# Six of eleven gate passes of an MLP up-projection written as seven block products, and the normed x split before them

## The chip, the cores and the metric

The kernel runs on one core of a Trainium2 chip. The metric is the device time of one execution in microseconds (us), the median of several runs; less is better. Engines are named as in the profile: PE is TensorE (matmuls), PEld its weight loads, DVE is VectorE, ACT is ScalarE, POOL is GpSimd, SP is SyncE, which issues the big loads. Each engine executes its own instructions in order and waits on semaphores for the others.

## The reference

Two layers of a decoder trunk on 512 tokens of width 1024, all in float32. Layer 0 mixes tokens by windowed attention and a short convolution, layer 1 by gated linear attention (GLA). Each layer goes on with an MLP and a small gated embedding. The change is in the MLP:

```python
DFF = 2816
def _conv_ffn(h, w_up, conv_w, conv_b, w_down):      # h = rms_norm(x) : 512 x 1024
    u = _causal_depthwise_conv(h @ w_up, conv_w) + conv_b   # w_up: 1024 x 5632, width-3 taps over the tokens
    gate, up = jnp.split(u, 2, axis=-1)                     # 2816 gates, 2816 values
    return (jax.nn.gelu(gate, approximate=False) * up) @ w_down
def _rms_norm(x, gain):
    return x * rsqrt(mean(x * x) + 1e-6) * gain
```

## The kernel before

Activations lie transposed in SBUF: features on the 128 partitions, the 512 tokens along the free side. `self.xT[0..7]` is the residual, 8 tiles of 128 features. A float32 product is made of three matmuls on rounded parts: each operand is split into a high part (a cast by ACT) and a low part (the difference, by DVE), and `mm3` (L157 to L159) adds high·high, high·low and low·high in one bank of PSUM. Weights are split where they are loaded: `weights` issues the load on SP into a tile `raw` (two buffers), and `cut` makes `wh` (ACT, L137) and `wl` (DVE, L138) from it, 1024 elements per partition at a time (three buffers each). A product whose weights are not cut yet waits; so does a cut whose buffer still holds weights that PE reads.

The MLP (`ffn`, one call for each layer `i`) runs 11 passes `d`. A pass loads 256 gate columns and 256 value columns of `w_up` (1 MB each) and makes four column blocks of 128 features (two gates, two values), each with 8 x 3 matmuls of 128 weights columns by 512 tokens, into one bank from `ps()` (four banks; `pa()` gives four others). The rms factor is left out of the matmuls' input: `xg` holds split tiles of x·gain, and the token factor R (from `spread`, a tile of 128 x 512) is multiplied in when a bank is read. `taps` does that (L785), starts the convolution on ACT (L786) and adds two shifted multiples on DVE (L788). Then come Gelu (L810), the product of gate and value (L813) and its split into high and low part (L101, L102), which feeds the down projection:

```python
for w, ps, fo in ((wg, pss[0], f), (wv, pss[1], NF + f)):
    y = taps(ps, fo)
    if w is wg:
        nc.scalar.activation(y, y, AF.Gelu)
    got.append(y)
g, y = got
nc.vector.tensor_tensor(y, g, y, ALU.mult)
self.split(acts[f], y)
```

The factor R exists only some time after the first column: the squares of x are summed over partitions by PE (L323), and `spread` uses DVE, ACT and PE (L335 to L346).

The order of instructions on each engine is chosen at build time by a scheduler from priorities and its own estimates of durations; inside `manual_schedule(engines=...)` it is the written order for the engines named. Buffers are handed out at build time too, with waits for the last reader. After the MLP of layer 1 comes `ple1`, which already computes a product by seven blocks (L945 to L947), some of its matmuls 256 columns wide.

Of the kernel before, what the change touches and what calls it, by code (L numbers as in the profile page):

```python
# [9 lines left out]
F32 = mybir.dt.float32  # L10
F32R = mybir.dt.float32r
I32 = mybir.dt.int32
U8 = mybir.dt.uint8
AF = mybir.ActivationFunctionType
ALU = mybir.AluOpType
# [3 lines left out]
P = 128  # L19
S = 512  # L20
D = 1024
NT = S // P
ND = D // P
DFF = 2816
NF = DFF // P
# [3 lines left out]
ET = mybir.EngineType  # L29
LEVELS = (64, 32, 16, 8, 4, 2, 1)  # L30
CW = 512
TWO_PI = 2.0 * np.pi
PI_SAFE = 3.1415925

# [22 lines left out]
class Kernel:  # L57
# [140 lines left out]
    def columns(self, name, views, q=None):  # L198

        nc = self.nc  # L200
        n = sum(v.shape[0] for v in views)
        rows = self.sp.tile([P, P], F32, tag="vrow", name=self.nm("vrow"))
        if q is None and self.gate is not None:
            self.late(rows[:, :1])
        at = 0
        for v in views:
            (q or nc.gpsimd).dma_start(rows[at : at + v.shape[0], :], v)
            at += v.shape[0]
        if q:

            nc.scalar.copy(self.few(4, "rs", 4), self.mhalf[:, :4])
        col = self.cp.tile([P, -(-n // 64) * 64], F32, name=name)[:, :n]

        def finish():
            ps = self.pa()
            nc.tensor.transpose(ps[:, :n], rows[:n, :], self.ident[:n, :n])
            (nc.vector.tensor_copy if q else nc.scalar.copy)(col, ps[:, :n])
            return col

        return finish if q else finish()  # L220
# [109 lines left out]
    def spread(self):  # L330
# [7 lines left out]
        for i, x in enumerate((rh.bitcast(F32), rl)):  # L338
# [5 lines left out]
            nc.tensor.matmul(pr, self.ones_r, dg.rearrange("p a b -> p (a b)"), start=i == 0, stop=i == 1)  # L344
        R = self.sp.tile([P, S], F32, tag="R", name=self.nm("R"))
        nc.scalar.copy(R, pr)  # L346
        return R

# [31 lines left out]
    def rope_tables(self, pool):  # L380
# [16 lines left out]
        c2 = 4058 * 2.0**-21  # L397
        c3 = TWO_PI - c1 - c2
        magic = 1.5 * 2.0**23
        sc = []  # L400
        for name, quarter in (("sin", 0.0), ("cos", 0.25)):
            kk = pool.tile([P, NT * h], F32, tag="kk", name=f"kk{name}")
            o = pool.tile([P, NT, h], F32, name=f"tab{name}")
            r = o.rearrange("p a b -> p (a b)")
            nc.vector.tensor_scalar(kk, af, 1.0 / TWO_PI, quarter, op0=ALU.mult, op1=ALU.add)
            nc.vector.tensor_scalar_add(kk, kk, magic)
# [4 lines left out]
            if quarter:  # L411
                nc.vector.tensor_scalar_add(r, r, TWO_PI * quarter)
            nc.vector.tensor_scalar(r, r, PI_SAFE, -PI_SAFE, op0=ALU.min, op1=ALU.max)
# [21 lines left out]
    def mixer0(self):  # L435
        nc, a, tc = self.nc, self.a, self.tc
        with tc.tile_pool(name="m0", bufs=1) as mp:
# [236 lines left out]
            def conv_w(nme, j2):  # L674
                c0 = starts[nme] + 256 * j2
                return self.weights(w_in[:, :, c0 : c0 + 256], ND, 256)
# [26 lines left out]
            def conv_out(j2):  # L703
                for c in range(2):
                    xs, y = pre[c]
                    nc.vector.tensor_tensor(xs, pss["b", c], R, ALU.mult)
                    nc.vector.tensor_tensor(y, y, xs, ALU.mult)
# [5 lines left out]
            w = conv_w("x", 0)  # L713
            R = self.spread()
            qn0 = query(0)
# [5 lines left out]
            self.gate = None  # L721
            R2 = self.sp.tile([P, S], F32, tag="R", name="R2")
            nc.gpsimd.tensor_tensor(R2, R, R, ALU.mult)
# [43 lines left out]
            self.end_norm()  # L767


    def ffn(self, i, next_gain):  # L770
        nc, a, tc = self.nc, self.a, self.tc
        xg, R = self.xg, None
        wu = a["ffn_w_up"][i].rearrange("(k p) n -> p k n", p=P)
        w0, w1, w2, bb = self.fcv
        with tc.tile_pool(name=f"ffn{i}", bufs=1) as fp:
            acts = [self.pair(self.fp, "b0", "b1") for f in range(8)]
            for f in range(8, NF, 2):
                four = self.four(fp)
                acts += [(four[:, 0], four[:, 1]), (four[:, 2], four[:, 3])]

            def taps(ps, f):
                y = fp.tile([P, S], F32, tag="zt", name=self.nm("zt"), bufs=4)
                z = fp.tile([P, S + 2], F32, tag="z", name=self.nm("z"), bufs=3)
                nc.gpsimd.memset(z[:, :2], 0.0)
                nc.vector.tensor_tensor(z[:, 2:], ps, R, ALU.mult)  # L785
                nc.scalar.activation(y, z[:, 2:], AF.Identity, scale=w2[:, f : f + 1], bias=bb[:, f : f + 1])  # L786
                for tap, w in ((1, w1), (0, w0)):
                    nc.vector.scalar_tensor_tensor(  # L788
                        out=y, in0=z[:, tap : tap + S], scalar=w[:, f : f + 1], in1=y, op0=ALU.mult, op1=ALU.add
                    )  # L790
                return y

            for d in range(NF // 2):
                wg = self.weights(wu[:, :, 256 * d : 256 * d + 256], ND, 256)
                wv = self.weights(wu[:, :, DFF + 256 * d : DFF + 256 * d + 256], ND, 256)
                for c in range(2):
                    f = 2 * d + c
                    got = []
                    pss = []
                    for w in (wg, wv):  # L800
                        ps = self.ps()
                        for k in range(ND):
                            self.mm3(ps, w(k, c * P, (c + 1) * P), xg[k], start=k == 0, stop=k == ND - 1)
                        pss.append(ps)
                    if R is None:
                        R = self.spread()
                    for w, ps, fo in ((wg, pss[0], f), (wv, pss[1], NF + f)):
                        y = taps(ps, fo)
                        if w is wg:
                            nc.scalar.activation(y, y, AF.Gelu)  # L810
                        got.append(y)
                    g, y = got
                    nc.vector.tensor_tensor(y, g, y, ALU.mult)  # L813
                    self.split(acts[f], y)
            self.begin_norm(("a0", "a1"))
            done = self.residual(next_gain)
            if i == 1:
                self.forms = []
                scratch = lambda: fp.tile([P, S], F32, tag="zt", name=self.nm("gx"), bufs=4)

                def done(m, ps):
                    nc.vector.tensor_tensor(self.xT[m], self.xT[m], ps, ALU.add)
                    self.blocks(m, next_gain, scratch)

            self.project(self.rows(a["ffn_w_down"][i]), acts, ND, done)
            if i == 0:
                self.end_norm()
            else:
                self.ple1(fp)
# [69 lines left out]
    def ple1(self, fp):  # L899
# [3 lines left out]
        nc, a, tc = self.nc, self.a, self.tc  # L903
        forms = self.forms
        wg = a["ple_w_gate"][1].rearrange("(j u p) n -> u p j n", p=P, u=2)
        wp = a["ple_w_proj"][1].rearrange("(k p) n -> p k n", p=P)
        sl = lambda hl, t: (hl[0][:, t * P : (t + 1) * P], hl[1][:, t * P : (t + 1) * P])
        H, J = D // 2, ND // 2
# [40 lines left out]
        def back(hf, t):  # L949

            pb = self.pa()
            for q in range(4):
                nc.tensor.transpose(
                    pb[:, q * P : (q + 1) * P], self.xT[4 * hf + q][:, t * P : (t + 1) * P], self.ident
                )
            x = fp.tile([P, 512], F32, tag="zt", name=self.nm("xt"), bufs=4)
            nc.scalar.copy(x, pb)
            return x

# [10 lines left out]
        def result():  # L970
            return fp.tile([P, S + 2], F32, tag="z", name=self.nm("so"), bufs=3)[:, :S]
# [14 lines left out]
        def finish(hf, t, g, x, pj, s=None, c0=0, c1=H):  # L986
            if s is None:
                s = result()[:, c0:c1]
            nc.scalar.activation(s, g, AF.Sigmoid, scale=self.r[:, t : t + 1])
            nc.vector.tensor_tensor(s, s, pj[:, c0:c1], ALU.mult)  # L990
            nc.vector.tensor_tensor(s, s, x[:, c0:c1], ALU.add)
            nc.sync.dma_start(self.out[0, t * P : (t + 1) * P, hf * H + c0 : hf * H + c1], s)

        b11 = block(0, 0, True)
        w11 = chunks(b11)
        b12 = block(0, 1, True)
        pin = self.p_halves(1)
        b22 = block(1, 1, False)
        wj_raw = self.four(fp, F32)
        proj_load(1)  # L1000
        b21 = block(1, 0, False)
# [3 lines left out]
        X, Q = [[self.ps() for _ in range(2)] for _ in range(2)]  # L1005
        both = (0, H)
        with tc.manual_schedule(engines={ET.PE, ET.DVE, ET.Activation}):
# [3 lines left out]
            steps = [(j, i, both, Q[i]) for j in range(J) for i in range(2)]  # L1011
# [13 lines left out]
            steps = [(j, i, both, X[i]) for j in range(J) for i in range(2)]  # L1025
# [15 lines left out]
            steps = [(j, i, both, Q[i]) for j in range(J) for i in range(2)]  # L1041
# [8 lines left out]
            halves = ((0, H // 2), (H // 2, H))  # L1050
            Y = [Q[0]] + [y[:, : H // 2] for y in (Q[1], X[0])]
# [4 lines left out]
            steps = [(j, i, both, X[i]) for j in range(J) for i in range(2)]  # L1056
# [476 lines left out]
```

## Time and profile before

| | |
|---|---|
| median of 3 runs | 1247.56 us (1247.32 to 1248.36) |
| profiled execution, its own time | 1248.2 us |
| its span in the trace | 1246.4 us |
| PE busy | 1236.1 us, 5984 matmuls |
| DVE busy | 804.6 us, 1251 instructions |
| ACT busy | 561.5 us, 873 instructions |
| granted TensorE clock | 1.0 |
| `ps<-a,wh` etc., L157 to L159, 128x512 | 3 x 864 matmuls, the up-projection among them |
| `z<-ps,R` (L785), 128x512, DVE | 88, mean 687 ns |
| `zt<-z,vfb` (L786), 128x512, ACT | 88, mean 808 ns |
| `zt<-z,vfa,zt` (L788), 128x512, DVE | 176, mean 749 ns |
| `wh<-raw` (L137), 128x1024, ACT | 176, mean 1061 ns |
| `wl<-raw,wh` (L138), 128x1024, DVE | 176, mean 1224 ns |
| load of 1 MB of `w_up` | 44, median 5.1 us from issue to landing |

The span is the time from the first to the last instruction of one profiled execution; its own time also has what lies around the span. A duration in the trace is that of one instruction alone. Instructions of one engine overlap a little at their ends, so the time from start to start is shorter than the duration when they follow each other without a wait. In the timeline a row begins with the start (us from the span's start) and the duration, then engine, line, operation, output and inputs, shape and count, and in brackets the idle time before it and what ended it. In a row of windows there are the stretch, its length, busy time and count for PE, PEld, DVE, ACT and POOL, then the granted clock, the share of the DMA engines and GB/s.

### The profile page before, as it was taken

What the parts mean: (1) busy time and instruction counts of PE and PEld (TensorE: products, weight loads), DVE (VectorE), ACT (ScalarE), POOL (GpSimd) and SP (SyncE); (2) the same over time, 40 slices, a digit from 0 to 9 for tenths busy, and PEclk for the clock granted to TensorE, in tenths of its full rate; (3) what the DMA queues carried; (4) which work ended last, traced back from release to release, by engine and by line L of the source; (5) the groups of instructions that cost most, each with busy time, mean ns of one, the idle gap of its engine ahead of it and who ended that gap; (6) DMA issues with size and microseconds to landing.
All of it is one profiled execution on the core that took longest, in us unless ns stands there. A gap on an engine that the chain in (4) does not pass through costs nothing.

```text
span 1246.4 us, 15216 instructions
## 1 busy us (share of the span) xinstructions
PE 1236.1 (99%) x5984; PEld 1023.9 (82%) x5984; DVE 804.6 (65%) x1251; ACT 561.5 (45%) x873; POOL 52.1 (4%) x152
## 2 busy tenths in 40 slices
PE   9999999999999999999999999999999999999998
PEld 8877788888888888888987878888888888888887
DVE  6886556777777633346679875557777777444495
ACT  7466344444444322234563554335444444333374
POOL 2500000000000000000100000000000000000000
PEclk9999999999999999999999999999999999999999
DMA  6222232233333232223322222332223333322411
GB/s 214 92 80 56 83 102 83 88 100 102 101 102 101 83 103 93 93 74 103 111 91 68 69 68 68 101 110 95 83 94 102 101 101 102 101 93 94 149 46 68
DMA packets 111004, 117.45 MB, mean 94 GB/s; under 512 B 2728, under 2 KB 106210, under 8 KB 110932
## 3 DMA queue, kind: packets, MB, share of 16 engines
q1 hardware_dynamic: 109568, 115.35, 28.4%
q8 instruction: 47, 0.77, 0.2%
q0 software_dynamic: 560, 0.42, 0.2%
q10 hardware_dynamic: 804, 0.70, 0.2%
q14 instruction: 25, 0.20, 0.0%
HBM read 114.37 MB, written 2.10 MB: 93 GB/s over the span
## 4 chain that ended last, share of the span: by engine, by line
PE 88%; DVE 7%; ACT 2%; issue 1%; POOL 1%; DVEq 0%; ACTq 0%; POOLq 0%
PE ps L157 26%; PE ps L158 26%; PE ps L159 26%; DVE wl L138 1%; PE ps L947 1%; PE ps L946 1%; PE ps L945 1%; PE pa L1367 1%; PE pa L1344 0%; PE pa L595 0%; PE pa L158 0%; PE pa L192 0%; PE pa L159 0%; DVE F L1228 0%; PE pa L157 0%
## 5 line engine op out<-in xcount | busy, mean ns | idle before, releaser
L137 ACT ACTIVATE wh<-raw 128x1024 fp32r<-128x1024 f32 (+4 forms) x212 | 214.2, 1012 | 333.3 <-PE ps L158 298.7
L138 DVE TENSOR_TENSOR wl<-raw,wh 128x1024 fp32r<-128x1024 f32 (+4 forms) x212 | 246.5, 1164 | 153.2 <-ACT wh L137 152.1
L157 PE MATMUL ps<-a,wh 128*128 128x512 f32 x864 | 336.9, 390 | 0.0
L158 PE MATMUL ps<-a,wh 128*128 128x512 f32 x864 | 336.6, 390 | 0.0
L159 PE MATMUL ps<-a,wl 128*128 128x512 f32 x864 | 336.3, 389 | 0.0
L158 PEld LDWEIGHTS ps<-a,wh 128*128 128x128 f32 x864 | 162.3, 188 | 34.0 <-issue 0.3
L159 PEld LDWEIGHTS ps<-a,wl 128*128 128x128 f32 x864 | 162.2, 188 | 33.9
L157 PEld LDWEIGHTS ps<-a,wh 128*128 128x128 f32 x864 | 162.2, 188 | 33.7 <-issue 0.7
L788 DVE SCALAR_TENSOR_TENSOR zt<-z,vfa,zt 128x512 f32<-128x512 f32 x176 | 131.3, 749 | 3.6 <-ACT zt L786 0.6
L157 PE MATMUL ps<-b,wh 128*128 128x512 f32 x320 | 126.0, 395 | 0.5 <-ACT b L101 0.5
L159 PE MATMUL ps<-b,wl 128*128 128x512 f32 x320 | 125.7, 393 | 0.0
L158 PE MATMUL ps<-b,wh 128*128 128x512 f32 x320 | 125.0, 391 | 0.0
L785 DVE TENSOR_TENSOR z<-ps,R 128x512 f32<-128x512 f32 x88 | 60.3, 687 | 74.7 <-PE ps L159 74.7
L157 PE MATMUL ps<-four,wh 128*128 128x512 f32 x224 | 87.1, 389 | 0.0
L158 PE MATMUL ps<-four,wh 128*128 128x512 f32 x224 | 87.1, 389 | 0.0
L159 PE MATMUL ps<-four,wl 128*128 128x512 f32 x224 | 87.1, 389 | 0.0
L786 ACT ACTIVATE zt<-z,vfb 128x512 f32<-128x512 f32 x88 | 70.9, 808 | 5.0 <-DVE z L785 3.3
L157 PEld LDWEIGHTS ps<-b,wh 128*128 128x128 f32 x320 | 60.0, 188 | 14.0 <-ACT b L101 1.3
L159 PEld LDWEIGHTS ps<-b,wl 128*128 128x128 f32 x320 | 60.1, 188 | 12.5
L158 PEld LDWEIGHTS ps<-b,wh 128*128 128x128 f32 x320 | 60.1, 188 | 12.5
L810 ACT ACTIVATE zt<-zt 128x512 f32<-128x512 f32 x44 | 27.8, 631 | 74.9 <-DVE zt L788 74.8
L101 ACT ACTIVATE four<-zt 128x512 fp32r<-128x512 f32 x28 | 17.7, 632 | 77.3 <-DVE zt L813 77.3
(359 smaller groups left out, 1555.0 us busy)
## 6 DMA issues: line engine op xcount, KB each, us to landing
raw<-in_ffn_w_up_dram SPq DMA_DIRECT2D x44, 1024.0 KB, 5.1
raw<-in_ffn_w_down_dram SPq DMA_DIRECT2D x16, 1024.0 KB, 4.7
raw<-in_hy_w_in_dram SPq DMA_DIRECT2D x8, 1024.0 KB, 5.0
raw<-in_gla_w_in_dram SPq DMA_DIRECT2D x8, 1024.0 KB, 5.3
raw<-in_ffn_w_down_dram SPq DMA_DIRECT2D x8, 768.0 KB, 4.1
raw<-in_ple_w_gate_dram SPq DMA_DIRECT2D x6, 1024.0 KB, 4.7
raw<-in_gla_w_out_dram SPq DMA_DIRECT2D x4, 1024.0 KB, 4.8
raw<-in_gla_w_in_dram SPq DMA_DIRECT2D x4, 672.0 KB, 4.0
```

Source lines behind the costliest of these rows:

```text
L101: nc.scalar.activation(h, src, AF.Copy)
L137: nc.scalar.activation(hv, v, AF.Copy)
L138: nc.vector.tensor_tensor(lv, v, hv.bitcast(F32), ALU.subtract)
L157: mm(out, lh, rh, start=start, stop=False)
L158: mm(out, lh, rl, start=False, stop=False)
L159: mm(out, ll, rh, start=False, stop=stop)
L785: nc.vector.tensor_tensor(z[:, 2:], ps, R, ALU.mult)
L786: nc.scalar.activation(y, z[:, 2:], AF.Identity, scale=w2[:, f : f + 1], bias=bb[:, f : f + 1])
L788: nc.vector.scalar_tensor_tensor(out=y, in0=z[:, tap : tap + S], scalar=w[:, f : f + 1], in1=y, op0=ALU.mult, op1=ALU.add)
L810: nc.scalar.activation(y, y, AF.Gelu)
L945: mm(o, lh, rh, start=first and j == 0, stop=False, **kw)
L946: mm(o, lh, rl, start=False, stop=False, **kw)
```

## The change

In passes `d` = 4 to 9 (`SEVEN = (4, 10)`) the two gate columns are no longer two sums of 8 x 3 matmuls of 512 tokens. The product of a 1024 x 256 block of weights with 1024 x 512 of the normed x is taken as a product of 2 x 2 blocks (even and odd tiles of features, two columns, two halves of the tokens) and made of seven block products, each of 4 x 3 matmuls of 256 tokens, with sums and differences of blocks on both sides. The weights' differences are made by DVE in the `raw` tile (`seven_forms`), those of x once in each layer (`sums`, in passes 0 and 1: two feature pairs `j` in each). Results that go into several outputs are copied between banks by ACT (`seven`). The gate products are interleaved with the value columns by hand: the first of them lies between the matmuls of the value column that the pass begins with (`begin`), the others among those of the second value column.

For this x must be normed before the matmuls: `sums` multiplies by R too and leaves the normed tiles in `scratch`; at the end of pass 3 `normed` splits them into the buffers of `xg`, tile by tile as PE leaves the old ones, and the taps of pass 3 are done after that (`finish`). From pass 4 on the taps read the banks directly. The padding of `z` and its memsets on POOL are gone (the shifted sums are 511 and 510 long). The products of gate and value are kept as float32 (`kept`); they are split only at the end of pass 9 (the first eight, into the buffers that held the sums) and after pass 10 in the text of the program (the rest). In layer 1 `ple1` gets its scratch tiles as halves of the new two-part tiles.

```diff
+SEVEN = (4, 10)
...
+    def sums(self, j, gain, R, scratch):
+        nc = self.nc
+        H = S // 2
+        for u in range(2):
+            m = 2 * j + u
+            nc.vector.scalar_tensor_tensor(
+                out=scratch[:, u], in0=self.xT[m], scalar=gain[:, m : m + 1], in1=R, op0=ALU.mult, op1=ALU.mult
+            )
+        e, o, s12, s34 = (scratch[:, u] for u in range(4))
+        out = []
+        nc.vector.tensor_tensor(s12[:, :H], e[:, H:], o[:, H:], ALU.add)
+        nc.vector.tensor_tensor(s12[:, H:], s12[:, :H], e[:, :H], ALU.subtract)
+        nc.vector.tensor_tensor(s34[:, :H], e[:, :H], e[:, H:], ALU.subtract)
+        nc.vector.tensor_tensor(s34[:, H:], o[:, :H], s12[:, H:], ALU.subtract)
+        for x in (s12, s34):
+            hl = self.pair(self.fp, "b0", "b1")
+            self.split(hl, x)
+            for c in (slice(0, H), slice(H, S)):
+                out.append((hl[0][:, c], hl[1][:, c]))
+        return out
...
+    def seven_forms(self, raw):
+        nc = self.nc
+        (b11, b12), (b21, b22) = self.blocks_of(raw)
+        plain = self.cut_blocks(raw[:, :, :P])
+        nc.vector.tensor_tensor(b11, b12, b11, ALU.subtract)
+        nc.vector.tensor_tensor(b12, b22, b12, ALU.subtract)
+        t13 = self.cut_blocks(raw.rearrange("p (j u) n -> p j u n", u=2)[:, :, 0])
+        nc.vector.tensor_tensor(b11, b22, b11, ALU.subtract)
+        t2 = self.cut_blocks(b11, False)
+        nc.vector.tensor_tensor(b21, b21, b11, ALU.subtract)
+        return plain, t13, t2
...
+    def seven(self, raw, ws, xg, forms):
...
+        product(W[:, left], plain, 0, tokens(0, 0), True)
+        nc.scalar.copy(X[:, left], W[:, left])
+        nc.scalar.copy(Y[:, left], W[:, left])
+        yield
+        product(V, t13, 0, s1, True)
+        more = self.sp.tile([P, S], F32, tag="acc", name=self.nm("more"), bufs=1)[:, :H]
+        nc.scalar.copy(more, V)
+        product(X[:, left], plain, 1, tokens(1, 0))
+        product(Y[:, left], t2, 0, s2)
+        nc.scalar.copy(X[:, right], Y[:, left])
+        yield
+        last = self.cut_blocks(raw.rearrange("p (j u) n -> p j u n", u=2)[:, :, 1])
+        product(X[:, right], t13, 1, s3)
+        nc.scalar.copy(Y[:, right], X[:, right])
+        yield
+        product(Y[:, left], last, 1, s4)
+        product(X[:, right], last, 0, tokens(1, 1))
+        yield X, Y, more
...
+            def begin(d, steps, w):
+                ps = self.pa()
+                value(w, ps, 0, 6)
+                next(steps)
+                value(w, ps, 6, ND)
+                return lambda y: taps(y[:, 1], ps, NF + 2 * d + 1)
...
+                if first <= d < last:
+                    with tc.manual_schedule(engines={ET.PE}):
+                        next(steps)
+                        V0 = self.pa()
+                        value(w0c, V0, 0, ND // 2)
+                        next(steps)
+                        value(w0c, V0, ND // 2, ND)
+                        X, Y, more = next(steps)
+                        mine = late
+                        if d + 1 < last:
+                            steps, w1c, w0c = prepare(d + 1)
+                            late = begin(d + 1, steps, w1c)
+                        mine(y)
+                        taps(y[:, 0], V0, NF + 2 * d)
+                        taps(g[:, 0], X, 2 * d)
+                        taps(g[:, 1], Y, 2 * d + 1, more)
+                        nc.scalar.activation(g, g, AF.Gelu)
...
+                    if d == first - 1:
+                        xg = normed(scratch)
+                        with tc.manual_schedule(engines={ET.PE}):
+                            steps, w1c, w0c = prepare(first)
+                            late = begin(first, steps, w1c)
+                        for f in todo:
+                            f()
...
+                nc.vector.tensor_tensor(u, g, y, ALU.mult)
+                for j in {0: (0, 1), 1: (2, 3)}.get(d, ()):
+                    forms.append(self.sums(j, gain, R, scratch[j]))
+                if d == last - 1:
+                    for f in range(8):
+                        hl = self.pair(self.fp, "b0", "b1")
+                        self.split(hl, at(f))
+                        acts.append(hl)
+            for d in range(4, NF // 2):
+                split_pair(y if d == NF // 2 - 1 else kept[d // 2][:, 2 * (d % 2) : 2 * (d % 2) + 2])
```

`product(out, w, c, x)` runs over the four feature pairs `j` and adds the three matmuls of each; `cut_blocks` is `cut` for blocks (a cast by ACT, a difference by DVE); `prepare(d)` loads both raw tiles of a pass, cuts the second value column and makes the weights' forms. Pass 10 and passes 0 to 3 keep their four plain columns.

## The prediction

> **What bounds the kernel now.** I read the engine table first, then the chain that ended last, then TensorE's waits, and last the order in time of single engines inside the MLP.
>
> ```profile
> PE 1236.1 (99%) x5984; PEld 1023.9 (82%) x5984; DVE 804.6 (65%) x1251; ACT 561.5 (45%) x873; POOL 52.1 (4%) x152
> ...
> PE 88%; DVE 7%; ACT 2%; issue 1%; POOL 1%; DVEq 0%; ACTq 0%; POOLq 0%
> ```
>
> TensorE is busy 99% of the 1246.4 us span and carries 88% of the chain. Its list of waits adds up to about 6 us, none over 1.5 us and none inside the MLP. So each microsecond taken from its matmuls is one gained, and each microsecond that it newly waits is lost for good. The pace of a matmul is its start-to-start time, from the timeline of TensorE:
>
> ```profile
> 227.68 0.39 PE L159 MATMUL ps<-a,wl 128*128 128x512 f32 x1
> ...
> 231.30 0.39 PE L157 MATMUL ps<-a,wh 128*128 128x512 f32 x1
> ...
> 1239.30 0.28 PE L945 MATMUL ps<-wh,a 128*128 128x256 f32 x1
> ...
> 1242.06 0.28 PE L947 MATMUL ps<-four,b 128*128 128x256 f32 x1
> ```
>
> The first pair is 16 matmuls apart: 0.2267 us for 512 columns. The second is 23 apart: 0.120 us for 256, each with its own weight load. Half the columns cost 53% of the time.
>
> Now VectorE (DVE) and ScalarE (ACT) where the MLP of layer 0 begins, and VectorE in the GLA stage:
>
> ```profile
> 196.14 1.06 ACT L137 ACTIVATE wh<-raw 128x1024 fp32r<-128x1024 f32 x1 [4.39 <-PE ps L158]
> 197.11 0.57 ACT L346 COPY R<-pa 128x512 f32<-128x512 f32 x1
> ...
> 198.38 1.28 DVE L785 TENSOR_TENSOR z<-ps,R 128x512 f32<-128x512 f32 x2
> 199.95 2.78 DVE L788 SCALAR_TENSOR_TENSOR zt<-z,vfa,zt 128x512 f32<-128x512 f32 x4 [0.29 <-ACT zt L786]
> ...
> 371.82 1.23 DVE L138 TENSOR_TENSOR wl<-raw,wh 128x1024 fp32r<-128x1024 f32 x1 [0.23 <-ACT wh L137]
> 372.96 1.53 DVE L788 SCALAR_TENSOR_TENSOR zt<-z,vfa,zt 128x512 f32<-128x512 f32 x2
> ...
> 645.89 0.42 DVE L1235 TENSOR_TENSOR F<-F,kT 128x256 f32<-128x256 f32 x1
> 646.23 0.42 DVE L1236 TENSOR_TENSOR F<-F,qT 128x256 f32<-128x256 f32 x1
> ```
>
> Queued work costs start to start, less than its duration. VectorE: 0.605 us for a 512-wide two-input operation (1.28 - 0.69 for the pair, and two of L340 in a row), 0.677 for a tap ((2.78 - 0.749) / 3), 1.14 for a 1024-wide one (371.82 to 372.96), 0.334 for a 256-wide one. ScalarE: 0.97 for 1024 (196.14 to 197.11), 0.54 for a 512-wide cast or Gelu, 0.71 for a tap's start. How full VectorE is in the first two passes (d = 0, 1) of layer 0, from the windows:
>
> ```profile
> 184.27:229.20 44.93, 44.93 (x203) 37.20 (x202) 31.33 (x42) 21.15 (x27) 1.73 (x8) 1.00 0.28 94
> ```
>
> 31.3 of 44.9 us, and until R exists (197.7) it can't start on any tap. Here is the least room in the MLP, and here the change puts `sums`.
>
> **Part by part.** *TensorE's work.* A pass has 96 matmuls of 512 columns, 21.76 us. In d = 4 to 9 the gates' 48 become 7 products x 12 matmuls of 256: 48 x 0.2267 + 84 x 0.120 = 20.96. That is 0.80 saved per pass, 12 passes: -9.6 us, all of it on the path.
>
> By the Trainium skill (TensorE: Matmul & The Clock Gate, Back-to-back issue gap) a warm matmul takes N/2.4 ns + 2.5 when isolated; estimated from that, a pass would save 1.19 and the kernel 14.2 us. This trace has 10.8 ns more at either width, and the rows decide.
>
> *Inside a seven-product pass.* By the built order VectorE has 8 taps, 5 low parts of 1024 and one of 512, 4 block differences, one add and the 1024-wide gate product: 5.4 + 5.7 + 0.6 + 2.4 + 0.6 + 1.1 = 15.9 of 20.96 us. ScalarE has 5 casts, a half cast, 4 taps, a Gelu and 5 copies of 256 (0.28 at most apart, from L1371's 0.38): about 10.6. The copies between banks lie behind 2.7 us of values each (12 x 0.2267), the first two behind 2.8. The tightest loop is a buffer: the raw gates stay until their last cut, so the next values' load, queued behind it on SyncE, starts some 12.1 us into the pass, lands 5.1 us later (median of the DMA table), is cast by 18.2 and is wanted at 20.96. I cost all this at nothing, with 2.8 us of cover; past that, each microsecond is paid 10 times. The POOL memsets that go were on no path.
>
> *The split of the normed x in d = 3.* A tile of x comes free every 0.68 us of the last column; ScalarE needs 0.54 and VectorE 0.605 for its halves, and `finish` is put off behind them. The first value column then wants one every 0.68. Nothing; without this cover up to 5 us a layer.
>
> *`sums` in d = 0 and 1.* VectorE executes in order, and in the built order the low part of d = 2's first gate weights (wl, first half of the pass) stands behind all four pairs' sums but one difference and two low parts. From R on it must first do 8 products with R, 16 taps, 3 low parts of weights, 2 gate products, 8 products x·gain·R, 15 operations of 256 and 6 low parts, and then that one: 4.84 + 10.83 + 4.56 + 2.28 + 5.42 + 5.01 + 3.63 = 36.6 us. Started at 198.4, that ends at 235.0 at the earliest. It has waits of its own too: 1.4 us for ScalarE's tap of the third column, 0.5 for the fourth column, 0.4 for a cast, 0.2 where one operation feeds the next. So 237.5. TensorE reaches d = 2 at 229.3 and finds only six matmuls that don't need a low part (two in each of three banks, 1.36 us; the built order puts exactly those first). Then it waits until 237.5: about **7.0 us**. Bounds: 4.4 without those waits, 9 if they double. Nothing behind makes it up. Both layers have this order: +14.0.
>
> *The splits of the activations, gathered at the end of d = 9.* Eight 512-wide and six 1024-wide ones stand among d = 9 and 10. Counted from d = 10's start, ScalarE still casts the last b halves until 1.0 (they wait for the last s4 product), then two taps (2.4), two weight casts (4.3), a 1024 split (5.3), a Gelu (6.3) and the last weight cast (7.3). TensorE ends the first column at 5.44, does four more matmuls to 6.35, wants that cast and waits 1.0. VectorE can do the gate product only after that Gelu: 7.5, a low part, then wl of the gates' second half at 9.4. TensorE waits again from 7.8: 1.6. Together **2.6 us** a layer, +5.2. The trace has no such crowd, so bounds: 0 if ScalarE is two operations ahead of this count, 5 if as much behind. The down projection finds its weights and splits ready.
>
> *Sum.* -9.6 + 14.0 + 5.2 = +9.6 us. The profiled execution took 1248.2 (span 1246.4 and 1.8 around it), 0.6 over the median of the runs, 1247.56. So 1257.8 as profiled, **1257.2** as a median.
>
> **Rivals.**
> *TensorE comes back at a slow pace.* At the kernel's start seven 512-wide matmuls of L192 take 3.35 us, some 0.45 each, twice the later pace; the longest wait afterwards, 1.5 us, leaves no such mark. A gap of over 6 us in d = 2 exists nowhere in this trace. If it brings the half pace back for 3.4 to 5 us, 1.6 to 2.4 us are lost in each layer: 1260.4 to 1262. For: the start; against: nothing but that the trace never tried. The Trainium skill (the same page, Part 1: The HAM clock gate) says just this: half clock after about 3.4 us idle, full again after about 3.4 us busy; by that rule the lower of the two. No run here shows it yet.
> *The sums stay hidden (the other side).* If VectorE gets through them by 230.6, the 7 us vanish and 1243.2 is left, 1238.0 if d = 10 holds no wait either. It decides at 32 us for the queue that I count at 36.6. For: the page's mean load of VectorE is 65%; against: that mean mixes stages, the order is fixed, and the sum alone is 4.4 us too long.
> *The raw-buffer loop binds.* If loads land 4 us later than the median, ten waits of about 1 us: 1267. Against: 28% load on the DMA engines.
> *The change doesn't save.* A weight load is shown with 188 ns; if it set the pace of 256-wide matmuls, each pass would lose 84 x 0.068 = 5.7 us, 68 in all: 1325. Against: 24 in a row at 0.120.
>
> **Numbers.** The forecast 0.48, the slow pace 0.32, hidden sums 0.11 (a third of it ending near no change), the buffer loop 0.06, weight loads 0.03. The two likely cases with the bounds of both stalls give 1249 (9.6 less 2 x 4.4 and little in d = 10) to 1264. Differences of under 0.2%, 2.5 us, can't be told from none here: faster 0.08, same 0.05, slower 0.87.
>
> **What would show it.** TensorE's busy time falls by some 10 us and a new idle sum of about 19 us appears, with `wl` low parts as releaser at two places of each MLP: 6 to 8 us where d = 2 begins (VectorE without a gap from 198 to 237), and two waits of 1 to 2 us in d = 10. A 12-matmul product lasts 1.44 us. The half pace would show as 0.43 us between 512-wide starts right behind the long gap. I am wrong if d = 2 starts without a gap, or if waits stand between the passes 4 to 9.

## The result, and the profile after

The changed kernel takes 1263.51 us (median of 4 runs, 1262.7 to 1264.68) beside 1247.76 for the kernel before (4 runs, 1247.32 to 1248.36): a ratio of 1.0127, with a 95% interval of 1.0109 to 1.0144. The profiled execution took 1262.7, with a span of 1260.9: 14.5 us more than the profiled execution of before by either measure. The prediction said 1257.2 (1249 to 1264).

The page of the changed kernel, its engine table, the row of granted clock and the chain:

```profile
PE 1232.8 (98%) x6416; PEld 1037.9 (82%) x6416; DVE 850.0 (67%) x1323; ACT 604.2 (48%) x963; POOL 44.1 (3%) x64
...
PEclk9999999899999999999999999999899999999999
...
PE 79%; DVE 13%; ACT 5%; issue 2%; POOL 1%; DMA 0%; ACTq 0%; DVEq 0%; POOLq 0%
```

TensorE is busy only 3.3 us less than before although its work shrank by more, VectorE has 13% of the chain instead of 7%, and the clock drops in two slices of the span, one in each MLP. The list of TensorE's waits over the whole span (total, times, longest) begins with two lines that the kernel before does not have:

```profile
PE ps L160 <- DVE wl L139: 15.6, 4, 6.5
PE ps L158 <- ACT wh L138: 1.8, 4, 0.5
```

Four waits for a low part of weights: two of 6.5 us where d = 2 begins, two of 1.3 in d = 10. Four waits of 0.4 to 0.5 us for a cast lie just ahead of them. The timeline of TensorE at d = 2 of layer 0 (start, duration, instruction, idle time before it and its releaser):

```profile
228.67 0.39 PE L159 MATMUL ps<-a,wh 128*128 128x512 f32 x1
229.53 0.50 PE L158 MATMUL ps<-a,wh 128*128 128x512 f32 x1 [0.47 <-ACT wh L138]
...
230.34 0.40 PE L159 MATMUL ps<-a,wh 128*128 128x512 f32 x1
237.23 0.80 PE L160 MATMUL ps<-a,wl 128*128 128x512 f32 x1 [6.50 <-DVE wl L139]
237.82 0.63 PE L158 MATMUL ps<-a,wh 128*128 128x512 f32 x1
238.25 0.63 PE L159 MATMUL ps<-a,wh 128*128 128x512 f32 x1
...
240.32 0.39 PE L158 MATMUL ps<-a,wh 128*128 128x512 f32 x1
240.55 0.39 PE L159 MATMUL ps<-a,wh 128*128 128x512 f32 x1
```

The timeline of VectorE just before the first low part:

```profile
235.61 0.42 DVE L784 TENSOR_TENSOR four<-four 128x256 f32<-128x256 f32 x1
235.94 1.23 DVE L139 TENSOR_TENSOR wl<-raw,wh 128x1024 fp32r<-128x1024 f32 x1
```

VectorE works without a break through 230 to 237, the sums' 256-wide operations right ahead of the `wl` that TensorE wants; this `wl` ends at 237.17 (235.94 + 1.23; predicted 237.5). Then the matmuls start 0.43 us apart until 240.3, and 0.23 apart from there. The windows of the same place, and of its twin in layer 1, have the stretch and its length, the busy time of the five engines, the granted clock in the third column from the right, and what the DMA engines did:

```profile
230.57:233.41 2.84, 0.16 (x1) 0.00 (x0) 2.84 (x6) 1.17 (x3) 0.00 (x0) 1.00 0.00 0
233.41:237.23 3.82, 0.00 (x1) 0.01 (x1) 3.82 (x7) 0.63 (x1) 0.00 (x0) 0.50 0.00 0
237.23:240.24 3.01, 3.01 (x7) 2.43 (x8) 3.01 (x5) 0.63 (x1) 0.00 (x0) 0.50 0.02 5
885.36:887.29 1.93, 0.00 (x1) 0.00 (x1) 1.93 (x5) 0.63 (x1) 0.00 (x0) 0.50 0.00 0
887.29:892.18 4.89, 4.89 (x12) 3.83 (x13) 3.75 (x5) 0.63 (x1) 0.00 (x0) 0.50 0.35 92
```

The clock goes to half while TensorE still waits and stays there for 3.0 us of work in layer 0 and 4.9 in layer 1: 1.5 and 2.4 us lost.

In d = 10 of layer 0 TensorE waits for a cast and a low part, and VectorE makes that low part (the first of the last row's three) behind splits of activations:

```profile
414.10 0.50 PE L158 MATMUL ps<-a,wh 128*128 128x512 f32 x1 [0.45 <-ACT wh L138]
416.15 0.50 PE L160 MATMUL ps<-a,wl 128*128 128x512 f32 x1 [1.32 <-DVE wl L139]
...
411.32 1.89 DVE L103 TENSOR_TENSOR b<-four,b 128x512 fp32r<-128x512 f32 x3
414.88 3.49 DVE L139 TENSOR_TENSOR wl<-raw,wh 128x1024 fp32r<-128x1024 f32 x3
```

Last, the gain, in TensorE's timeline of the first product of d = 4:

```profile
285.00 0.28 PE L842 MATMUL pa<-a,wh 128*128 128x256 f32 x1
...
286.31 0.28 PE L844 MATMUL pa<-a,wl 128*128 128x256 f32 x1
286.43 0.40 PE L158 MATMUL pa<-a,wh 128*128 128x512 f32 x1
```

Twelve matmuls in 1.43 us (predicted 1.44). From the first product of d = 4 to that of d = 5 (306.04) the pass takes 21.04 us, and no wait stands between d = 4 and d = 9.

By start-to-start times of TensorE the difference is then, over both layers: 12 passes x -0.72 = -8.6; the gap at d = 2, 2 x 7.4 = +14.8 (the waits of 6.50 and 0.47, and some 0.4 lost at restarts); half clock +3.9; d = 10, 2 x 2.3 = +4.6. Sum +14.7; the spans differ by 14.5. The fit is closer than the account deserves: the slow matmuls at the start of the kernel end at a different moment in each profile, so that the one matmul of L388 (L389 after), long before the change, starts at 23.32 us before and at 22.52 after. Behind that place the difference is 15.3 us, and 0.6 of it no term of the sum explains.

### The profile page after: what moved, and what is told of

Read it like the earlier page. It is cut to its first block, busy times and chain, and to the rows that moved or that the text cites. A ratio compares the mean times of both kernels' runs of the same rounds, so it can differ in the third digit from the quotient of the medians.

```text
span 1260.9 us, 16071 instructions
## 1 busy us (share of the span) xinstructions
PE 1232.8 (98%) x6416; PEld 1037.9 (82%) x6416; DVE 850.0 (67%) x1323; ACT 604.2 (48%) x963; POOL 44.1 (3%) x64
## 4 chain that ended last, share of the span: by engine, by line
PE 79%; DVE 13%; ACT 5%; issue 2%; POOL 1%; DMA 0%; ACTq 0%; DVEq 0%; POOLq 0%
PE ps L160 17%; PE ps L158 17%; PE ps L159 17%; PE pa L159 4%; PE pa L158 4%; PE pa L160 4%; DVE wl L139 2%; PE ps L843 2%; PE ps L842 2%; PE ps L844 2%; DVE zt L896 2%; DVE b L103 1%; PE ps L1166 1%; PE ps L1164 1%; PE ps L1165 1%
## 5 line engine op out<-in xcount | busy, mean ns | idle before, releaser
L138 ACT ACTIVATE wh<-raw 128x1024 fp32r<-128x1024 f32 (+4 forms) x188 | 188.4, 1005 | 339.7 <-PE ps L159 287.5
L139 DVE TENSOR_TENSOR wl<-raw,wh 128x1024 fp32r<-128x1024 f32 (+4 forms) x188 | 216.8, 1156 | 183.7 <-ACT wh L138 183.3
L160 PE MATMUL ps<-a,wl 128*128 128x512 f32 x480 | 187.8, 394 | 15.6 <-DVE wl L139 15.6
L158 PE MATMUL ps<-a,wh 128*128 128x512 f32 x480 | 189.5, 395 | 1.8 <-ACT wh L138 1.8
L159 PE MATMUL ps<-a,wh 128*128 128x512 f32 x480 | 188.5, 393 | 0.0
L160 PEld LDWEIGHTS ps<-a,wl 128*128 128x128 f32 x480 | 91.1, 190 | 36.4 <-DVE wl L139 17.4
L158 PEld LDWEIGHTS ps<-a,wh 128*128 128x128 f32 x480 | 91.2, 190 | 22.5 <-ACT wh L138 3.5
L159 PEld LDWEIGHTS ps<-a,wh 128*128 128x128 f32 x480 | 91.1, 190 | 19.0 <-issue 0.3
L158 PE MATMUL pa<-a,wh 128*128 128x512 f32 x192 | 75.3, 392 | 0.0
L159 PE MATMUL pa<-a,wh 128*128 128x512 f32 x192 | 75.3, 392 | 0.0
L160 PE MATMUL pa<-a,wl 128*128 128x512 f32 x192 | 74.7, 389 | 0.0
L158 PEld LDWEIGHTS ps<-b,wh 128*128 128x128 f32 x320 | 60.0, 188 | 14.2 <-ACT b L102 1.3
L896 DVE SCALAR_TENSOR_TENSOR zt<-z,vfa,zt 128x511 f32<-128x511 f32 (+1 forms) x88 | 64.8, 748 | 5.5 <-ACT zt L894 5.0
L807 ACT ACTIVATE wh<-raw 128x1024 fp32r<-128x1024 f32 x36 | 38.0, 1057 | 36.9 <-DVE raw L820 20.2
```

Source lines behind the costliest of these rows:

```text
L138: nc.scalar.activation(hv, v, AF.Copy)
L139: nc.vector.tensor_tensor(lv, v, hv.bitcast(F32), ALU.subtract)
L158: mm(out, lh, rh, start=start, stop=False)
L159: mm(out, lh, rl, start=False, stop=False)
L160: mm(out, ll, rh, start=False, stop=stop)
L807: nc.scalar.activation(h, src, AF.Copy)
```

## The experiments

The theory: the sums' place in VectorE's order makes the gap, the gap makes the half clock, the crowd of splits makes the waits of d = 10, and the rest is the gain of the seven products. In the first four runs the kernel before took 1247.71 us, in the last three 1247.75.

**Sums spread.** 

```diff
-                for j in {0: (0, 1), 1: (2, 3)}.get(d, ()):
+                for j in {0: (0,), 1: (1,), 2: (2, 3)}.get(d, ()):
```

> The sums of pair 0 stay in pass d = 0, pair 1 goes to d = 1, pairs 2 and 3 to d = 2; nothing else changes. Theory (the gap at d = 2 is VectorE's queue, and the slow matmuls behind it are the price of the gap): before the wl that d = 2 waits for, two pairs fewer are queued, 7.8 us, so that it ends some 8 us earlier, near 229, before TensorE wants it at 230.7. Both the gap (7.4 us a layer in start-to-start times) and the slow matmuls (1.5 and 2.4 us) vanish: 18.7 us less than the changed kernel's 1263.5, 1244.8. First rival (the queue only moves the wait on): pass d = 2 holds the two pairs now, and a wait of 3 to 7 us a layer appears where d = 3 begins or in d = 4: 1250 to 1260. Second rival (the slow pace has a cause of its own in d = 2, not the gap): the gap goes, the slow matmuls stay: 1248.7.

Measured: 1252.13 us, ratio 1.0041 (1.0027 to 1.0055): 11.4 less than the changed kernel, not 18.7. At d = 2 there is no wait and no half clock, so the gap was VectorE's queue, and the second rival is out. The first rival holds in part: TensorE now waits in d = 4, in layer 0 so:

```profile
280.85 0.39 PE L842 MATMUL pa<-b,wh 128*128 128x256 f32 x1 [0.83 <-ACT wh L807]
...
282.10 0.38 PE L844 MATMUL pa<-b,wl 128*128 128x256 f32 x1 [0.76 <-DVE wl L808]
...
285.71 0.39 PE L844 MATMUL ps<-b,t 128*128 128x256 f32 x1 [0.48 <-DVE t L808]
```

These are waits for the cast and the low part of the second product's weights and for the low part of `t2`: together 2.85 us a layer from start to start (2.1 for the first two), 5.7 in all. The waits of d = 10 stayed, and in layer 1 they now brought one step of half clock, 1.7 us. 18.7 less 5.7 and 1.7 is 11.3, against 11.4 measured.

**Splits later.**

```diff
-                if d == last - 1:
+                if d == last:
                     for f in range(8):
```

> The eight 512-wide splits of the first activations are issued behind pass d = 10's own work instead of at the end of d = 9; nothing else changes. Theory (ScalarE and VectorE serve these splits ahead of the weight cuts of d = 10, and TensorE waits for the cuts): the waits in d = 10, 2.3 us a layer in start-to-start times, vanish: 1263.5 - 4.6 = 1258.9. Rival (the work is too much for the pass wherever it stands): VectorE has 26 us of work for 21.8 us of d = 10, and the down projection waits for the last splits instead, 0 to 4 us a layer: 1259 to 1267.

Measured: 1258.23 us, ratio 1.0087 (1.0073 to 1.01), 5.3 below the changed kernel. TensorE waits nowhere in d = 10 or in the down projection of either layer. The theory holds, and the work fits when it stands behind the pass's own. One wait of 0.5 us for `t2` is new, in the passes of layer 0.

**Both moved.** The two edits together.

> The two moves together: sums of the pairs in d = 0, 1 and twice in d = 2, the eight splits behind d = 10's work. Theory: only TensorE's saving is left, 12 passes x 0.72 us (21.76 less the 21.04 that the trace after shows) = 8.6 us below the kernel before, 1247.8 - 8.6 = 1239.1 (1263.5 - 18.7 - 4.6 = 1240.2 the other way round). Rival (the moves collide, since both load VectorE later): 1243 to 1250, with a new wait in d = 3, 4 or the down projection.

Measured: 1245.91 us, ratio 0.9987 (0.9978 to 0.9995): the rival. TensorE's timeline at the second product of d = 4, layer 0:

```profile
279.28 0.39 PE L160 MATMUL pa<-a,wl 128*128 128x512 f32 x1
280.49 0.39 PE L842 MATMUL pa<-b,wh 128*128 128x256 f32 x1 [0.82 <-ACT wh L807]
280.72 0.28 PE L843 MATMUL pa<-b,wh 128*128 128x256 f32 x1
281.75 0.39 PE L844 MATMUL pa<-b,wl 128*128 128x256 f32 x1 [0.76 <-DVE wl L808]
```

The windows of that place, columns as above:

```profile
279.07:282.47 3.40, 1.82 (x11) 1.19 (x10) 2.82 (x4) 3.02 (x4) 0.00 (x0) 1.00 0.00 0
282.47:285.88 3.41, 3.41 (x19) 3.41 (x18) 3.41 (x6) 0.91 (x2) 0.00 (x0) 0.50 0.53 172
```

Two waits of 0.8 us (2.1 from start to start), and then 3.41 us of half clock without any gap, in both layers. Waits of 2.1 and half a step, 1.7, make 3.8 a layer, 7.6 in all: -8.6 + 7.6 = -1.0. The spans differ by -1.3 (1245.1 against 1246.4), of which 0.3 is the start of the kernel (23.02 against 23.32 for the early matmul named above). The profiled execution is one of three in eleven with a mean granted clock of 0.997 (1246.9 to 1247.2 us); the other eight show 0.999 or 1.0 and took 1244.6 to 1246.3. Two steps of half clock are 0.0027 of the span, so the other eight cannot have had both of them.

What is late is VectorE:

```profile
278.61 0.68 DVE L820 TENSOR_TENSOR raw<-raw 128x512 f32<-128x512 f32 x1
...
279.38 1.06 ACT L807 ACTIVATE wh<-raw 128x1024 fp32r<-128x1024 f32 x1
```

The cast that TensorE waits for follows VectorE's difference of weight blocks, which ends at 279.29. VectorE works from 254.5 to 279.9 with one break of 0.35 us, first the two pairs' sums of d = 2, then the splits of the normed x.

**Gap filled.**

```diff
+                    if d == 2:
+                        with tc.manual_schedule(engines={ET.PE}):
+                            self.nowhere = self.pa()
+                            self.idle(28)
                     wg = self.weights(wu[:, :, gates(d)], ND, 256)
```

> 28 matmuls of 512 columns on a constant, into a bank that nobody reads, stand on TensorE ahead of pass d = 2 in each layer; nothing else changes. They last 28 x 0.2267 = 6.35 us and fill the gap but for about 1 us; the time of the gap itself isn't given back, since VectorE sets its end. Theory (the slow pace is the price of TensorE's idleness): the matmuls behind run at 0.227 us from start to start at once, and 1.5 + 2.4 = 3.9 us are won: 1259.6. Rival (the slow pace comes from something else at that place, such as the weights' reads or VectorE's queue): the slow starts stay, 1263.5.

Measured: 1260.5 us, ratio 1.0103 (1.0089 to 1.0117), 3.0 below the changed kernel. TensorE's timeline behind what is left of the gap:

```profile
237.62 0.50 PE L160 MATMUL ps<-a,wl 128*128 128x512 f32 x1 [0.92 <-DVE wl L139]
237.96 0.40 PE L158 MATMUL ps<-a,wh 128*128 128x512 f32 x1
238.19 0.40 PE L159 MATMUL ps<-a,wh 128*128 128x512 f32 x1
```

The `wl` comes when it came, and the matmuls run 0.23 us apart at once: TensorE's idleness was the cause of the slow pace. In the profiled run the waits of d = 10 in layer 0 cost a step of half clock instead (415.18 to 418.60, 1.7 us), which is why its span is only 2.2 us shorter, not 3.9.

**Sums even.** Both moves, and pair 2 back in d = 1:

```diff
-                for j in {0: (0,), 1: (1,), 2: (2, 3)}.get(d, ()):
+                for j in {0: (0,), 1: (1, 2), 2: (3,)}.get(d, ()):
```

> As the run with both moves, but pair 2 goes back to d = 1: one pair in d = 0, two in d = 1, one in d = 2. Theory (VectorE's order sets it at each end): by the same start-to-start prices the wl for d = 2 ends at 226.8 plus 2 to 3 us of waits, before 230.7, the wl of its first values at 234.1 plus the same 2 to 3, against 235.6: a wait of 0 to 1.5 us a layer there; and d = 3 begins with 3.9 us less on VectorE, so that the cut for the second product of d = 4, which came 1.9 us late, is in time. TensorE keeps most of the 8.6 us: 1239 to 1242, some 1240.5. Rival (the late cut in d = 4 comes from the eight splits of the normed x and not from the sums): the wait in d = 4 stays, and with it the half clock: 1245 to 1247.

Measured: 1241.49 us, ratio 0.9951 (0.9939 to 0.9964): faster than both kernels, 6.3 us below the one before and 22.0 below the changed one. Its engine table:

```profile
PE 1227.9 (99%) x6416; PEld 1035.5 (84%) x6416; DVE 848.6 (68%) x1323; ACT 604.7 (49%) x963; POOL 44.1 (4%) x64
```

TensorE's waits in the MLP of layer 0, the whole list:

```profile
PE ps L158 <- ACT wh L138: 0.5, 1, 0.5
```

TensorE's busy time falls by 8.2 us against before, close to the 8.6 that the seven products save. The one wait left in each MLP is the 0.47 us for a cast at d = 2, 0.8 from start to start. The profiled spans differ by 6.9 us, 0.7 of it at the start of the kernel; 8.6 less 2 x 0.8 would be 7.0 without that, and what takes the remaining 0.8 stays open. The late cut in d = 4 needed the second pair of sums in d = 2: with one pair the splits of the normed x are hidden.

**Three passes.** `SEVEN = (4, 7)` in place of `(4, 10)`.

> Only three passes of each layer (d = 4 to 6) take seven products, the other three are plain as before; sums, split of the normed x and the gathered splits all stay, the last now between d = 6 and d = 7. Theory (a pass saves 21.76 - 21.04 = 0.72 us and the rest is paid once): 6 x 0.72 = 4.3 us slower than the changed kernel, 1267.8. By the prediction's 0.80 a pass it would be 1268.3. Rival (passes 4 to 9 hold a cost of their own that the waits don't show): less than 1266, or faster than the changed kernel.

Measured: 1262.6 us, ratio 1.012 (1.0106 to 1.0134). The number missed the theory and met the rival, but the trace shows no hidden cost: the passes take 21.03 and 21.04 us here too. What the expectation left out is that d = 10's waits go. Here the eight 512-wide splits fall between d = 6 and 7, apart from the 1024-wide ones, and TensorE waits nowhere from d = 4 on: so either group alone is hidden, and the two together are the crowd. Half clock lasts longer in this profile (10.24 us in layer 1; 4.9 us are lost in both layers together, against 3.9): +4.3 - 4.6 + 1.0 = +0.7. The spans differ by +0.7 (1261.6 against 1260.9), but 0.6 of that is the start of the kernel (23.09 against 22.52 at L389), so the sum is good to some 0.6 us only.

**Gap half filled.** 14 matmuls in place of 28.

> As the run with the filled gap, with 14 constant matmuls instead of 28: they last 3.17 us, so that TensorE idles for about 3.4 of the 6.6 us ahead of the first low part in d = 2. Theory from the traces so far (the granted clock changes on a fixed grid of 3.413 us, and goes to half for one step after a step in which TensorE idled for more than about half): one step of half clock in each layer, 3.41 us long, part of it inside the gap; 0.3 to 1.7 us lost a layer, 1261 to 1263. Rival (half clock needs 3.4 us of idleness in one piece, counted from its start, and as long a busy time to come back): either no slow start at all, 1260.5 as with the filled gap, or a slow stretch of 3.4 us that begins exactly where the gap ends, 1263.5.

Measured: 1262.55 us, ratio 1.012 (1.0104 to 1.0135). A gap of 4.2 us from start to start was left, more than meant. The half clock lasts from 236.77 to 240.19 in layer 0 (one step of 3.42; the next matmul starts at 237.28, so it began inside the gap) and from 885.31 to 892.13 in layer 1 (two steps). The change points lie on the grid (worked out in the last section); that it would be one step in each layer was wrong.

## Why the prediction came out as it did

*The pace and the passes.* Right in kind, 1.0 us too large: -9.6 foreseen, -8.6 measured. The matmuls took 0.2267 and 0.120 as assumed; the sum left out what a change of width costs. Six 512-wide matmuls between products last 1.39 us instead of 1.36, twelve 2.75 instead of 2.72, and eighteen 4.11 instead of 4.08: 0.03 at each of four groups, less a little in the products, 0.08 in a pass. By the estimate from the Trainium skill's figure (TensorE: Matmul & The Clock Gate, Back-to-back issue gap) 14.2 us would have been won; no run supports that, the 256-wide matmuls stay at 0.12.

*Inside the passes.* Right for this kernel: no wait in d = 4 to 9, neither for the copies between banks nor for the raw buffer, and no load that sets the pace. The rivals "the raw-buffer loop binds" and "the change doesn't save" are out. The cover is not wide, as the wait of 0.5 us for `t2` in one layer of the run splits later shows.

*The split of the normed x.* "Nothing" holds for this kernel. The cover is thin: the low part for the second product of d = 4 ends at 286.19 and is wanted at 288.06. With two pairs of sums in d = 2 the second product is 2.1 us late (both moved); with one pair, 3.9 us less on VectorE, it is not (sums even).

*The sums.* The step was right: VectorE's queue, counted from start to start with its own waits, sets the end of the gap. From its first product with R (197.56) to the end of the `wl` (237.17) VectorE took 39.6 us, 39.1 foreseen. TensorE's gap is 7.4 us from start to start against about 7.0 (the prediction's own figures, 237.5 less 229.3 and 1.36, give 6.84). The listed waits, 6.50 and 0.47, add up to 6.97, but the 0.47 for a cast was not foreseen.

*The splits at the end of d = 9.* The place and the two waits were right, the size 2.3 a layer against 2.6; ScalarE's cast was wanted 0.6 us before it came, not 1.0. Moving the eight splits took all of it away.

*The slow pace.* Here the forecast failed: it was listed as a rival at 0.32 and left out of the likeliest case, at a price of 3.2 to 4.8 us for both layers; it came, at 3.9. With it the prediction's own sum is 9.6 + 3.9 = 13.5, against 14.5 measured in the profile; the other three terms missed by +1.0, +0.8 and -0.6, which partly cancel. The step that failed is "For: the start; against: nothing but that the trace never tried": nothing spoke against it, and so it belonged in the forecast. The lower of the two prices, 1.6 us a layer, fits layer 0 (1.5) but not layer 1 (2.4): the half clock lasts 6.83 us in both, but in layer 1 more of that falls behind the gap. The Trainium skill's rule (the same page, Part 1: The HAM clock gate), half clock after some 3.4 us idle, agrees with the 3.41 us of one step; that much idleness was not needed in these runs (both moved).

*The median.* It rose by 15.7 us, the profiled execution by 14.5: the four runs lie 2 us apart, and the two longer ones show the lower mean granted clock (0.993 against 0.995). One more step of half clock would be 0.0014 of the span and 1.7 us. That the steps fall differently in each run fits this; where they fell was seen only in the profiled ones. The likeliest figure, 1257.2, is 6.3 us too low, and that 1263.5 still lies inside the range, 0.5 us below its upper end, is partly luck: the prediction doesn't show how it reached 1264, and the upper bounds of its two stalls alone would give 1257.2 + 4.0 + 4.8 = 1266.0.

## What to carry to other kernels

Work for an idle engine is not free where the busy engine's next operand stands behind it in the same in-order queue: count that queue from start to start up to the one instruction that is waited for, pass by pass, and spread the new work until every such sum ends in time. Here the sums made gaps of 14.8 us in one place and waits of 1.6 us in another (sums even), and only then did 6.3 of the 8.6 us saved on TensorE reach the kernel's time. Where a gap of four microseconds or more is forecast on TensorE, put the half clock behind it into the sum, not among the rivals: it came behind every gap of 4.1 us or more that the MLPs of these runs show.

## What the runs showed of the hardware that was not expected

The granted clock changes on a fixed grid; a step here is one interval of it. In the changed kernel's profile half clock begins at 233.41 and 885.36; these are 651.95 us apart, 191.0 steps of 3.413 us. In the others the same quotient is 188.0 (both moved), 190.0 (gap half filled, three passes and splits later), and each stretch lasts one, two or three steps: 3.41, 6.83, 10.24 us.

No gap of 3.4 us is needed. Most steps of full clock in which TensorE was busy for 0 to 1.84 us of 3.41 were followed by half clock, even where that was two waits of 0.8 us (both moved); steps with 2.04 us or more were not. But one with 1.79 (878.53 to 881.94, changed kernel) and one with 1.71 (1233.70 to 1237.11, sums even) were not either, while steps with 1.83 and 1.84 were. So the busy time that the profile shows does not settle it between 1.7 and 1.9. A step of half clock with 2.59 us busy was followed by another one at half (three passes), steps with 2.91 (gap half filled) and 3.01 (changed kernel) by full clock. So two short waits in one step can cost 1.7 us more than they last, or nothing, by where they fall on the grid. What exactly is counted stays open.
